# The first load of a gated linear unit issued before the launch barrier in place of after it

## The chip, the cores and the metric

The kernel runs on one core of one Trainium2 chip. The metric is the device time of one execution in microseconds (us). Each kernel is run several times, and the kernel before is run again in the same rounds.

## The reference, cut to what matters

```python
def setup_inputs():
    return {"x": np.random.randn(8192, 8192).astype(np.float32)}

def reference(x):
    a, b = np.split(x, 2, axis=-1)
    return a * (1 / (1 + np.exp(-b)))      # 8192 x 4096, float32
```

268.44 MB are read and 134.22 MB are written. For each output element there is one sigmoid and one multiply.

## The kernel before

The input is worked in 32 tiles. A tile has two rows of x in each of the 128 partitions (64 KB per partition, 8.4 MB in all), and there are two buffers for the input tile and two for the output tile. SyncE issues the loads, ScalarE computes the sigmoid of the b half in place, VectorE multiplies, ScalarE issues the stores. Only the last tile is worked and stored in four pieces per row.

```python
pool = ctx.enter_context(tc.tile_pool(name="io", bufs=BUFS))        # 2
# ... cut: the variant with one row for each partition, not used ...
for i in range(n_tiles):                                            # 32
    x_sb = pool.tile([P, in_cols], fp32)
    o_sb = pool.tile([P, out_cols], fp32)
    eng(LOAD_ENG, i).dma_start(out=x_sb, in_=x_t[i])                # SyncE
    n_chunks = TAIL_CHUNKS if i >= n_tiles - TAIL_ITERS else 1      # 4 in the last tile
    for r in range(PAIR):                                           # 2
        # ... cut: the slices a_part, b_part, o_part ...
            nc.scalar.activation(out=b_part, in_=b_part, func=SIG)
            nc.vector.tensor_mul(out=o_part, in0=a_part, in1=b_part)
            # ... cut: in the last tile a store for each piece ...
    if n_chunks == 1:
        eng(STORE_ENG, i + 1).dma_start(out=out_t[i], in_=o_sb)     # ScalarE
```

One part of the program is not in this text. The framework puts an entry block ahead of the kernel's own instructions. In it GpSimd fills four small constants, and then all five engines meet at what is called the launch barrier here: each executes a drain (DRAIN in the profile) and signals its arrival through a semaphore, a counter that other engines can wait for; GpSimd waits for the four other arrivals and then releases all. The kernel's first load stands after this barrier.

## Time and profile before

| | before |
|---|---|
| time, median of the first runs | 936.99 us (936.17 to 937.19) |
| span of the profiled execution | 934.1 us |
| DMA engines | 9 tenths or more in 39 of 40 slices, 431 GB/s on average |
| VectorE, ScalarE busy | 30%, 25% |
| issue of the first load | 0.73 us after the start of the span |
| first sigmoid | 22.66 us |

The page of the profiled execution begins with the busy shares, the span in 40 slices (a digit is the busy share in tenths), the bytes moved, and the chain of waits that ended last.

```profile
...
DVE 280.9 (30%) x70; ACT 230.0 (25%) x71; POOL 0.2 (0%) x4
...
DMA  9999999999999999999999999999999999999998
...
DMA packets 10226, 402.67 MB, mean 431 GB/s; under 512 B 1136, under 2 KB 1136, under 8 KB 2160
...
## 4 chain that ended last, share of the span: by engine, by line
DMA 78%; DVE 15%; ACT 6%; issue 0%; DVEq 0%; ACTq 0%; SPq 0%
...
```

The compute engines are mostly idle, the DMA engines hardly ever. The Trainium skill, "DMA: Bandwidth & Descriptors", Specifications, gives a fabric ceiling of 435 GB/s, and the 431 GB/s of this trace agree with it. So the DMA engines bound the kernel, and with the same bytes to move, time can be won only where they are idle. That is at the two ends of the span. The head is the subject here.

This is the order of time of the head in the trace of before (start, duration, engine, line, operation; in brackets the idle time of the engine before it and what ended it).

```profile
...
0.73 1.28 ACT L84 ACT_TABLE_LOAD   x1 [0.73 <-PEq L106]
0.73 34.69 SPq L70 DMA_DIRECT2D x_sb<-in_x_dram  x3
22.66 7.12 ACT L84 ACTIVATE x_sb<-x_sb 128x4096 f32<-128x4096 f32 x2 [20.65 <-DMA x_sb<-in_x_dram]
26.31 8.76 DVE L85 TENSOR_TENSOR o_sb<-x_sb 128x4096 f32<-128x4096 f32 x2 [26.31 <-ACT x_sb L84]
...
```

Nothing is computed before 22.66 us. ScalarE is idle for 20.65 us and waits for the first load to land, that is for its last bytes to be in place.

These are the instructions of the barrier in the same trace. The columns are line, engine, operation, count, then the duration in ns (shortest, median, longest) and the first and the last start in us.

```profile
...
L106 POOLq EVENT_SEMAPHORE  x2: 17/17/17, 0.5 to 0.6; - x2
L106 SPq DRAIN  x1: 7/7/7, 0.0 to 0.0; - x1
...
L106 POOLq DRAIN  x1: 181/181/181, 0.3 to 0.3; - x1
L106 PEldq DRAIN  x1: 8/8/8, 0.3 to 0.3; - x1
...
L106 SPq EVENT_SEMAPHORE  x1: 17/17/17, 0.7 to 0.7; - x1
...
```

SyncE is there first, at 0.0 us. GpSimd, which has the four constants to fill, drains only at 0.3 us and releases the others with its semaphore instructions at 0.5 and 0.6 us. SyncE goes on at 0.7 us. In the view of what the DMA-issuing queue of SyncE waited for, this is the line of the launch (the profile names the engine whose arrival came last by its records, PE).

```profile
...
SPq L106 <- PEq L106: 0.7, 1, 0.7
...
```

So 0.7 us pass in which the core could have fetched data. The last line needed is that of the DMA engines in the first 3 us, in 40 slices of 0.075 us each.

```profile
...
DMA  0000000000000000000000099900909000090000
...
```

The first packets (pieces of a transfer, here 64 KB each) start in slice number 23, counted from zero. The view counts a packet in the slice in which it starts, so the zeros after it are not idle time: the same view gives the time of these 16 packets as 104.9% of the window.

### The profile page before, as it was taken

The page shows a single profiled execution, that of the slowest core. Times are in us where ns is not written, and L with a number is a line of the kernel's source. Part 1 is how long each engine was busy: PE and PEld are TensorE (multiplying, and loading weights), DVE is VectorE, ACT ScalarE, POOL GpSimd, SP SyncE. Part 2 cuts the span into 40 slices and gives each one's busy share as a digit, 9 for nine tenths or more (in the row PEclk, how much of TensorE's full clock was granted, in tenths as well). Part 3 has the DMA queues.
Part 4 walks back from the last instruction along what each step waited for, and adds up shares of the span by engine and source line. Part 5 has one row for each costly group of instructions (what it writes and reads, how often), then busy time and mean ns, then how long its engine had stood idle before and what let it go on. Part 6 is the DMA issues. An engine that isn't in the chain of part 4 may idle for free.

```text
span 934.1 us, 410 instructions
## 1 busy us (share of the span) xinstructions
DVE 280.9 (30%) x70; ACT 230.0 (25%) x71; POOL 0.2 (0%) x4
## 2 busy tenths in 40 slices
DVE  0333321333213332133321333312333123331234
ACT  0313331133311333113332033320233202333023
POOL 0000000000000000000000000000000000000000
DMA  9999999999999999999999999999999999999998
GB/s 404 404 449 427 427 449 427 427 434 464 404 441 434 428 449 425 451 408 462 410 429 446 425 450 420 453 408 453 421 429 446 424 452 429 441 411 450 424 449 359
DMA packets 10226, 402.67 MB, mean 431 GB/s; under 512 B 1136, under 2 KB 1136, under 8 KB 2160
## 3 DMA queue, kind: packets, MB, share of 16 engines
q1 hardware_dynamic: 4608, 268.44, 66.5%
q10 hardware_dynamic: 5616, 134.22, 33.3%
q14 instruction: 2, 0.02, 0.0%
HBM read 268.44 MB, written 134.22 MB: 431 GB/s over the span
## 4 chain that ended last, share of the span: by engine, by line
DMA 78%; DVE 15%; ACT 6%; issue 0%; DVEq 0%; ACTq 0%; SPq 0%
DMA x_sb<-in_x_dram 78%; DVE o_sb L85 15%; ACT x_sb L84 6%; DVEq L117 0%; ACTq L87 0%; SPq L70 0%; ACTq L84 0%
## 5 line engine op out<-in xcount | busy, mean ns | idle before, releaser
L85 DVE TENSOR_TENSOR o_sb<-x_sb 128x4096 f32<-128x4096 f32 (+1 forms) x70 | 280.9, 4056 | 647.3 <-ACT x_sb L84 647.3
L84 ACT ACTIVATE x_sb<-x_sb 128x4096 f32<-128x4096 f32 (+1 forms) x70 | 228.7, 3315 | 696.1 <-DMA x_sb<-in_x_dram 692.0
L84 ACT ACT_TABLE_LOAD x1 | 1.3, 1283 | 0.7 <-PEq L106 0.7
L106 POOL MEMSET const-bfloat16-1.0<- 128x1 bf16 x1 | 0.1, 102 | 0.0
L106 POOL MEMSET const-uint8-127<- 128x1 uint8 x1 | 0.1, 102 | 0.0
L106 POOL MEMSET const-float32-1.0<- 128x1 f32 x1 | 0.1, 99 | 0.0
L106 POOL MEMSET const-float32-0.0<- 128x1 f32 x1 | 0.1, 98 | 0.2 <-issue 0.2
## 6 DMA issues: line engine op xcount, KB each, us to landing
out_dram<-o_sb ACTq DMA_DIRECT2D x31, 4096.0 KB, 41.8
out_dram<-o_sb ACTq DMA_DIRECT2D x8, 512.0 KB, 6.3
x_sb<-in_x_dram SPq DMA_DIRECT2D x32, 45.5
```

What stands on the lines that cost most here:

```text
L84: nc.scalar.activation(out=b_part, in_=b_part, func=SIG)
L85: nc.vector.tensor_mul(out=o_part, in0=a_part, in1=b_part)
L106: nc = _bacc.Bacc("TRN2", target_bir_lowering=False, num_devices=1)
```

## The change

The intent is to issue the first load while the engines are still gathering. It has no input that the barrier protects and it waits for no semaphore. The source was rewritten without its dead options at the same time. The core of the diff, with the rewritten loop cut, is this:

```diff
 ... cut: the loop, rewritten as _tiles() with the same tiles, buffers and queues ...
+    with ExitStack() as pools:
+        _tiles(pools, tc, x, out)
+    tc.close()
+    tc.compile()
+    blocks = nc.main_func.blocks
+    entry, body = blocks[0].instructions, blocks[1].instructions
+    SP = mybir.EngineType.SP
+    at = next(k for k, i in enumerate(body) if i.engine == SP)
+    load = body[at]
+    assert load.opcode == "DMACopy" and not load.sync_info.on_wait
+    del body[at]
+    where = next(k for k, i in enumerate(entry) if i.engine == SP and i.opcode == "Drain")
+    entry.insert(where, load)
```

More of the change, by code (lines that the diff above doesn't have):

```diff
@@ L1 @@
-import os
 from contextlib import ExitStack
@@ L5, with _tiles @@
 import concourse.tile as tile
-from concourse import bass_utils, mybir
+from concourse import mybir
 from concourse._compat import with_exitstack
+def _tiles(ctx, tc, x, out):
+    nc = tc.nc
+    P = nc.NUM_PARTITIONS
+    fp32 = mybir.dt.float32
+    SIG = mybir.ActivationFunctionType.Sigmoid
+    n_rows, n_cols = x.shape
+    half = n_cols // 2
+    R = 2
+    n_tiles = n_rows // (P * R)
+    x_t = x.rearrange("(n p r) m -> n p (r m)", p=P, r=R)
+    out_t = out.rearrange("(n p r) m -> n p (r m)", p=P, r=R)
+    pool = ctx.enter_context(tc.tile_pool(name="io", bufs=2))
+    first = None
+    for i in range(n_tiles):
+        x_sb = pool.tile([P, R * n_cols], fp32)
+        o_sb = pool.tile([P, R * half], fp32)
+        load = nc.sync.dma_start(out=x_sb, in_=x_t[i])
+        first = first or load
+        n = 4 if i == n_tiles - 1 else 1
+        w = half // n
+        for r in range(R):
+            for c in range(n):
+                lo = r * n_cols + c * w
+                a = x_sb[:, lo : lo + w]
+                b = x_sb[:, lo + half : lo + half + w]
+                cols = slice(r * half + c * w, r * half + (c + 1) * w)
+                nc.scalar.activation(out=b, in_=b, func=SIG)
+                nc.vector.tensor_mul(out=o_sb[:, cols], in0=a, in1=b)
+                if n > 1:
+                    nc.scalar.dma_start(out=out_t[i, :, cols], in_=o_sb[:, cols])
+        if n == 1:
+            nc.scalar.dma_start(out=out_t[i], in_=o_sb)
+    return first
 @with_exitstack
@@ L17 @@
     nc = tc.nc
-    P = nc.NUM_PARTITIONS
-    PAIR = int(os.environ.get("GLU_PAIR", "2"))
-    BUFS = int(os.environ.get("GLU_BUFS", "2" if PAIR == 2 else "5"))
-    STORE_ENG = os.environ.get("GLU_STORE", "scalar")
-    LOAD_ENG = os.environ.get("GLU_LOAD", "sync")
-    TAIL_CHUNKS = int(os.environ.get("GLU_TAIL_CHUNKS", "4"))
-    TAIL_ITERS = int(os.environ.get("GLU_TAIL_ITERS", "1"))
-    n_rows, n_cols = x.shape
-    half = n_cols // 2
-    assert out.shape == (n_rows, half)
-    fp32 = mybir.dt.float32
@@ L32 @@
-    SIG = mybir.ActivationFunctionType.Sigmoid
-    def eng(name, i):
-        if name == "alt":
-            name = "sync" if (i % 2 == 0) else "scalar"
-        return getattr(nc, name)
-    pool = ctx.enter_context(tc.tile_pool(name="io", bufs=BUFS))
-    if PAIR == 1:
-        x_t = x.rearrange("(n p) m -> n p m", p=P)
-        out_t = out.rearrange("(n p) m -> n p m", p=P)
-        n_tiles = x_t.shape[0]
-        for i in range(n_tiles):
-            x_sb = pool.tile([P, n_cols], fp32)
-            eng(LOAD_ENG, i).dma_start(out=x_sb, in_=x_t[i])
-            n_chunks = TAIL_CHUNKS if i >= n_tiles - TAIL_ITERS else 1
-            csz = half // n_chunks
-            for c in range(n_chunks):
-                lo = c * csz
-                hi = lo + csz
-                a_part = x_sb[:, lo:hi]
-                b_part = x_sb[:, half + lo : half + hi]
-                nc.scalar.activation(out=b_part, in_=b_part, func=SIG)
-                nc.vector.tensor_mul(out=a_part, in0=a_part, in1=b_part)
-                eng(STORE_ENG, i + 1).dma_start(out=out_t[i, :, lo:hi], in_=a_part)
-    else:
-        x_t = x.rearrange("(n p r) m -> n p (r m)", p=P, r=PAIR)
-        out_t = out.rearrange("(n p r) m -> n p (r m)", p=P, r=PAIR)
-        n_tiles = x_t.shape[0]
-        in_cols = PAIR * n_cols
-        out_cols = PAIR * half
-        for i in range(n_tiles):
-            x_sb = pool.tile([P, in_cols], fp32)
-            o_sb = pool.tile([P, out_cols], fp32)
-            eng(LOAD_ENG, i).dma_start(out=x_sb, in_=x_t[i])
-            n_chunks = TAIL_CHUNKS if i >= n_tiles - TAIL_ITERS else 1
-            for r in range(PAIR):
-                a_all = x_sb[:, r * n_cols : r * n_cols + half]
-                b_all = x_sb[:, r * n_cols + half : (r + 1) * n_cols]
-                o_all = o_sb[:, r * half : (r + 1) * half]
-                csz = half // n_chunks
-                for c in range(n_chunks):
-                    lo = c * csz
-                    hi = lo + csz
-                    a_part = a_all[:, lo:hi]
-                    b_part = b_all[:, lo:hi]
-                    o_part = o_all[:, lo:hi]
-                    nc.scalar.activation(out=b_part, in_=b_part, func=SIG)
-                    nc.vector.tensor_mul(out=o_part, in0=a_part, in1=b_part)
-                    if n_chunks > 1:
-                        eng(STORE_ENG, i + 1).dma_start(
-                            out=out_t[i, :, r * half + lo : r * half + hi], in_=o_part
-                        )
-            if n_chunks == 1:
-                eng(STORE_ENG, i + 1).dma_start(out=out_t[i], in_=o_sb)
```

## The prediction

> **What bounds the kernel now.** The 16 DMA engines. The page's slices show DMA at 9 tenths in 39 of 40 slices; 402.67 MB moved at a mean of 431 GB/s. VectorE is busy 30% of the 934.1 us span, ScalarE 25%. The Trainium skill, "DMA: Bandwidth & Descriptors", Specifications, gives a fabric ceiling of 435 GB/s; the 431 GB/s agree. The chain that ended last is 78% loads and 21% the sigmoid and multiply between a load's landing and the next load into the same buffer, but while that chain is in VectorE the other buffer's load and the stores fill the DMA engines.
>
> **What the change does.** Arithmetic, tiles, buffers, queues and tail are the same. One instruction moves: the first load goes from behind the launch barrier to before SyncE's drain, which is SyncE's arrival at it.
>
> Sizes, from the instructions of the barrier's line and of the load's line. SyncE's drain is at 0.0 us, so SyncE reaches the barrier first; PE's and GpSimd's drains are at 0.3 us (GpSimd's takes 0.18 us, after four memsets), GpSimd's two semaphore instructions are at 0.5 and 0.6, and SyncE's release is at 0.7. The first load is issued at 0.73 us, its issue takes about 0.4 us (0.417 is the longest of the 32), and the data phase starts at 1.17 us in the chain of waits. All of this heads the chain: the sigmoid waits until 22.66 us for that load.
>
> Removed: at most 0.73 us, the release at which the first load stands. Added: SyncE's arrival at the barrier comes about 0.4 us later, but still before GpSimd's chain at 0.5 us, so the barrier should end where it did, or 0.1 us later. Moved: the second load is issued as the first instruction of SyncE after the barrier, at about 0.75 us instead of 1.15; it queues behind 8.4 MB that need about 20 us. ScalarE's table load stays at 0.73 us and ends at about 2.0. A drain doesn't wait for data: ScalarE's last one took 0.15 us while its stores needed about 6 us to land, so SyncE's should not wait for the load either.
>
> **How much shows.** All work after the first landing only follows its predecessors, so the whole schedule should be shifted, by 0.6 to 0.75 us: about 0.07%. The three runs of before spread over 1.0 us, so the gain is smaller than the spread of single runs.
>
> **Prediction.** 936.3 us, 8 in 10 between 934.9 and 937.4. Faster by over 2%: 0.005; within 2%: 0.99; slower by over 2%: 0.005.
>
> **What would show the steps right.** The first load's issue at 0.0 us; the data phase at about 0.45 us; the first sigmoid at about 21.95 us in place of 22.66; the barrier's release still at 0.7 to 0.8 us; the last multiply about 0.7 us earlier; load landings still 45.5 us (median), sigmoid 3.6 us and multiply 4.42 us, the same rate of about 431 GB/s; span about 933.4 us.
>
> **What would make it wrong.** The span's zero is the first instruction: if SyncE starts no earlier in real time and its first issue is slower, the gain shrinks to nothing. If SyncE's drain did wait for the data, the second load would be issued at about 22 us and the DMA engines would idle some 2 us between the two: slower by about 1 us. A different interleaving of loads and stores could move the total by a microsecond either way.

## The result, and the profile after

The changed kernel took 935.99 us (median of 5 runs, 935.59 to 936.31), against 936.99 us before (936.17 to 937.19, 5 runs). The ratio is 0.9992, with a 95% interval from 0.9980 to 1.0004; it is the mean time of one kernel's runs over that of the other's in the same rounds, so it is not quite the ratio of the medians. By its interval this pair alone does not tell a gain from none. Executions over 1.5% slower than the fastest of the same kernel are left out of the means. All outputs are right. The changed kernel's span is 933.9 us.

The page of the profiled execution after, with the lines that answer to those of before:

```profile
...
DVE 280.9 (30%) x70; ACT 230.0 (25%) x71; POOL 0.2 (0%) x4
...
DMA  9999999999999999999999999999999999999998
...
DMA packets 10226, 402.67 MB, mean 431 GB/s; under 512 B 1136, under 2 KB 1136, under 8 KB 2160
...
DMA 78%; DVE 15%; ACT 6%; issue 0%; DVEq 0%; ACTq 0%
...
```

None of these totals changed. The order of time of the head after:

```profile
...
0.00 34.73 SPq L28 DMA_DIRECT2D x_sb<-in_x_dram  x3
...
0.78 1.28 ACT L38 ACT_TABLE_LOAD   x1 [0.78 <-PEq L85]
21.96 7.12 ACT L38 ACTIVATE x_sb<-x_sb 128x4096 f32<-128x4096 f32 x2 [19.90 <-DMA x_sb<-in_x_dram]
25.61 8.76 DVE L39 TENSOR_TENSOR o_sb<-x_sb 128x4096 f32<-128x4096 f32 x2 [25.61 <-ACT x_sb L38]
...
```

The first load is issued at 0.00 us and the first sigmoid starts at 21.96 us in place of 22.66. The barrier's instructions after:

```profile
...
L85 POOLq EVENT_SEMAPHORE  x2: 17/17/17, 0.6 to 0.7; - x2
...
L85 POOLq DRAIN  x1: 181/181/181, 0.3 to 0.3; - x1
...
L85 SPq DRAIN  x1: 126/126/126, 0.4 to 0.4; - x1
L85 SPq EVENT_SEMAPHORE  x1: 17/17/17, 0.7 to 0.7; - x1
...
```

SyncE now drains at 0.4 us, behind the issue of the load. That drain takes 126 ns in place of 7, but it does not wait for the 8.4 MB, and GpSimd's release moves by less than 0.1 us. In the waits of SyncE's queue 0.2 of the 0.7 us are left:

```profile
...
SPq L85 <- PEq L85: 0.2, 1, 0.2
```

The DMA engines in the first 3 us after the start:

```profile
...
DMA  0000000000000999909900000000090000000000
...
```

The first packets start in slice 13, ten slices sooner than before. The same view of a window of 0.2 us, with finer slices, puts them at 1.00 us, and in before at 1.73: 0.73 us sooner. The Trainium skill, "DMA: Bandwidth & Descriptors", Latency and other measured facts, gives about 0.6 us to the first byte on the path that SyncE uses. The load's issue takes 0.376 us here, so the first packet comes 0.6 us after the end of the issue, which agrees, but 1.0 us after its start.

One thing in this pair of profiles does not fit a plain shift. These are the first sigmoids of the last tile, in the order of time of before and then of after:

```profile
...
914.83 2.95 ACT L84 ACTIVATE x_sb<-x_sb 128x1024 f32<-128x1024 f32 x3 [21.79 <-DMA x_sb<-in_x_dram]
...
914.69 2.95 ACT L38 ACTIVATE x_sb<-x_sb 128x1024 f32<-128x1024 f32 x3 [21.76 <-DMA x_sb<-in_x_dram]
...
```

The gain is 0.70 us at the first sigmoid of the kernel and only 0.14 us here (the expectations call this the last sigmoid), and the spans differ by 0.2 us. The median of five says 1.0 us. Whether the gain is kept, and whether it is the load's at all, had to be tried.

### The profile page after: what moved, and what is told of

Its sections match the earlier page's. It is cut to its first block, busy times and chain, and to the rows that moved or that the text cites. A ratio compares the mean times of both kernels' runs of the same rounds, so it can differ in the third digit from the quotient of the medians.

```text
span 933.9 us, 410 instructions
## 1 busy us (share of the span) xinstructions
DVE 280.9 (30%) x70; ACT 230.0 (25%) x71; POOL 0.2 (0%) x4
## 4 chain that ended last, share of the span: by engine, by line
DMA 78%; DVE 15%; ACT 6%; issue 0%; DVEq 0%; ACTq 0%
DMA x_sb<-in_x_dram 78%; DVE o_sb L39 15%; ACT x_sb L38 6%; DVEq L61 0%; ACTq L41 0%; ACTq L38 0%
```

## The experiments

Theory: only the start of the first load matters, and an earlier start shifts the whole schedule, because the DMA engines are busy from then on. Rivals: the difference comes from the rewrite or from chance; or the gain is used up in the saturated middle; or the second load's earlier issue has a part in it.

### The move undone, and the changed kernel again (e1, e2)

Kernel e1 is the changed kernel without the edit of the blocks. The built program has, instruction for instruction, those of before. Kernel e2 is the changed kernel.

```diff
-    blocks = nc.main_func.blocks
-    entry, body = blocks[0].instructions, blocks[1].instructions
-    ...
-    entry.insert(where, load)
```

> The rewritten source with the first load left behind the barrier. Theory (the move alone makes the gain, about 0.7 us, and it shifts the whole schedule): same as the kernel before, ratio within 0.9996 to 1.0004, first sigmoid at 22.6 to 22.7 us. Rival (the rewrite or the chip made the 1.0 us difference of the medians): the time of the changed kernel, about 0.999, although the first sigmoid stands at 22.66.

> The changed kernel once more, in the rounds of the undone one. Theory: 0.6 to 0.8 us under before and under the undone kernel (ratio 0.9991 to 0.9994), first sigmoid at 21.95 us, and the gain at the last sigmoid scattered around 0.7 us. Rival (the gain at the head is used up later by the saturated DMA engines, as the first pair of profiles suggests, 0.70 us at the first sigmoid and 0.14 at the last): first sigmoid at 21.95 us, but again only 0.0 to 0.3 us at the last one and in the time.

Measured: e1 936.42 us (median of 5; ratio to before 0.9997), first sigmoid at 22.50 us. Kernel e2 936.04 us (ratio 0.9992), first sigmoid at 21.96 us. Kernel before in the same rounds 936.75 us (9 runs). The means of the runs are 936.52, 936.05 and 936.77 us. The sign is the theory's, but not all that was expected came: e2 lies 0.72 us under before but only 0.47 under e1, e1's first sigmoid is 0.1 us sooner than expected, one run of e2 took 936.97 us, and e1 lay 0.25 us under a kernel with the same instructions. In the profile of e2 the last tile's first sigmoid starts at 914.73 us, only 0.10 us before that of before, as the rival said, and 0.30 before that of e1 (915.03). One profile of each is too little here. Over all kept profiles with the short barrier the load behind it gives 914.83 (before), 915.03 (e1) and 915.54 (e9), and the load ahead of it 914.69, 914.73 (e2) and, from experiments below, 914.30 (e5), but also 917.16 (e10). So before is the earliest of its kind, all profiles but e10 keep some of the gain to the last tile, and e10 is looked at below. At this size repetition alone answers slowly.

### The barrier made longer by a known amount (e3, e4)

If the load's place counts, then a longer barrier must make the difference larger. Ten memsets on GpSimd go ahead of its drain in the entry block, once in the undone kernel (e3) and once in the changed one (e4). The edit, shortened:

```diff
+    pad = ctx.enter_context(tc.tile_pool(name="pad", bufs=1)).tile([P, 1024], fp32)
+    for _ in range(10):
+        nc.gpsimd.memset(pad, 0.0)
 ...
+    for p in pads:                  # the ten memsets, taken out of the body
+        at = next(k for k, i in enumerate(entry) if i.engine == POOL and i.opcode == "Drain")
+        entry.insert(at, p)
```

> First load behind the barrier, and the barrier made longer by 10 memsets of 128x1024 on GpSimd ahead of its drain. They delay the release by D, to be read in this trace (D guessed at 10 us, between 5 and 20). Theory: the time grows by all of D, since the first load waits for the release: before plus D within 0.5 us. Rival (a delay at the head is used up later): clearly less than D.

> First load ahead of the same longer barrier. Theory: D is hidden whole as long as the release comes before the first load has landed (about 22 us), as the second load still queues behind the first: the time of the changed kernel within 0.5 us, that is D plus 0.7 us under the padded undone kernel; first sigmoid at about 22 us. Rival (the load's early start is worth only its own fixed 0.7 us, or the data does not flow before the barrier is over): the time grows by part or all of D.

The order of time of e3, load behind the barrier:

```profile
...
0.37 10.03 POOL L26 MEMSET pad<- 128x1024 f32 x10
...
10.71 34.57 SPq L31 DMA_DIRECT2D x_sb<-in_x_dram  x3
32.51 7.12 ACT L41 ACTIVATE x_sb<-x_sb 128x4096 f32<-128x4096 f32 x2 [20.53 <-DMA x_sb<-in_x_dram]
...
```

And of e4, load ahead of it:

```profile
...
0.00 56.23 SPq L31 DMA_DIRECT2D x_sb<-in_x_dram  x4
...
0.36 10.03 POOL L26 MEMSET pad<- 128x1024 f32 x10
...
21.87 7.12 ACT L41 ACTIVATE x_sb<-x_sb 128x4096 f32<-128x4096 f32 x2 [9.89 <-DMA x_sb<-in_x_dram]
...
```

In both the memsets run to about 10.4 us. In e3 the first load is issued at 10.71 us, 9.98 us later than in before, and the first sigmoid starts at 32.51. In e4 it is issued at 0.00 and the first sigmoid starts at 21.87 us, though SyncE stood 10.1 us at the barrier by its own waits:

```profile
...
SPq L95 <- PEq L95: 10.1, 1, 10.1
...
```

The times: e3 946.52 us (4 runs, ratio 1.0105), e4 936.03 us (5 runs, ratio 0.9992). The delay of 9.98 us costs e3 10.1 us against the mean of the undone kernel in the same rounds (946.58 less 936.52), and costs e4 nothing (936.00 against 936.05 for e2). Between e3 and e4 lie 10.58 us, where the first loads are issued 10.71 us apart. This is the finding that carries the rest, as it is far outside the scatter (the five runs of e1 lie within 0.66 us, those of e2 within 1.52): a delay of the first load of this size shifts the end one to one within about 0.1 us, nothing of it that these runs can tell is given back in the middle, and a load ahead of the barrier hides this barrier whole.

### Two loads ahead of the barrier (e5)

The edit is the same insertion, done twice.

> The first two loads both ahead of the short barrier. Theory (only the start of the first load matters; the second queues behind it for 20 us): the time of the changed kernel, ratio to before 0.9990 to 0.9996, first sigmoid at 21.9 to 22.0 us, second at 43.5 to 43.8; the barrier may end 0.3 us later, since SyncE now issues for about 0.8 us before its drain, and nothing shows of it. Rival (the second load's earlier issue is part of the gain): a further gain of about 0.4 us.

Measured: 935.68 us (5 runs, ratio 0.9992), first sigmoid at 22.03 us, second at 44.07. Their mean lies 0.81 us under before of the same rounds, and those of the changed kernel's first two sets 0.82 and 0.72 us under theirs. No further gain shows. The release moved to 1.25 us, 0.5 us later than in the changed kernel where 0.3 was expected, and both sigmoids are a little later than expected, the second by 0.3 us; none of this shows in the time.

### Where the hiding ends (e6, e7, e11)

The same memsets, 40 of them, with one load ahead of the barrier (e6) and with two (e7).

> First load ahead of a barrier of 40 memsets; release at about 40.6 us (10 memsets made 9.97 us). Theory: hiding ends where the first load has landed, at 21.9 us. The DMA engines idle from then to the issue of the second load at 40.6 us, 18.7 us: time of the changed kernel plus 18 to 20 us, about 955 us, in place of plus 40 where the load stands behind the barrier. First sigmoid at about 42 us, after the table load. A theory in which any barrier is hidden: plus 0. One in which only the head of the load is hidden: plus 39.

> Two loads ahead of the same 40 us barrier. Theory: the DMA engines work until both have landed at 43.5 us. The first sigmoid starts at about 42 us (table load after the release), so the first store and the third load are issued when VectorE has done the first tile, 12.4 us later, at about 54.4 us in place of 34.4. Idle DMA from 43.5 to 54.4 us, so plus 10 to 12 us: about 947 us. If the second load ahead of the barrier brings nothing, the time of the run with one load, about 955.

In the order of time of e6, these are the table load after the release and the first sigmoid:

```profile
...
40.95 1.28 ACT L41 ACT_TABLE_LOAD   x1 [40.95 <-PEq L95]
42.24 7.12 ACT L41 ACTIVATE x_sb<-x_sb 128x4096 f32<-128x4096 f32 x2
...
```

The stretches of e6 from 20 to 41 and from 41 to 42 us; the last two figures of a line are the share of the DMA engines and GB/s:

```profile
...
20.00:41.00 21.00, 0.00 (x0) 0.05 (x1) 19.49 (x21) 1.00 0.00 0
41.00:42.00 1.00, 0.00 (x0) 1.00 (x1) 0.00 (x0) 1.00 1.00 328
...
```

The first load landed at 21.9 us and the next packets come after 41 us. For some 20 us (21.9 to 41.9) the DMA engines have nothing to move. Kernel e6 took 956.79 us (2 runs), which is 20.8 us more than the changed kernel, against the 18 to 20 expected. What was short in the sum: the release came at 40.9 us in place of 40.6, and the second load needs another microsecond from its issue to its first packet. With both the sum is 20 us; the other 0.8 us is no more than single runs of other sets scatter, and its cause is not shown.

The two early loads of e7 are both issued within 0.4 us of the start. Their times from issue to landing:

```profile
...
DMA to landing us min/median/max: 22.0/31.4/40.8
```

The stretches of e7 between the second landing and the first store and third load:

```profile
...
41.00:55.00 14.00, 8.76 (x2) 8.39 (x3) 0.00 (x0) 1.00 0.00 0
55.00:56.00 1.00, 0.00 (x0) 0.86 (x1) 0.00 (x0) 1.00 2.82 786
...
```

Two loads with nothing beside them land at 40.8 us. The 43.5 us of the expectation were read from the changed kernel, where a third load and a store share the DMA engines from 34.4 us on. That made the idle stretch 14.8 us in place of 11. Kernel e7 took 954.01 us in its one fast run, 18.0 us more than the changed kernel, so 3 us beyond the idle stretch; its other run, 968.60 us, is listed as slow because it lies over 1.5% above the first, not for its granted clock, which is 1.0 too. It was run again:

> Two loads ahead of the 40 us barrier again, as one of its two runs was slow. The first profile had both loads landed at 40.8 us, since alone they are not slowed by a third load and a store as in the changed kernel (43.6), and the first packet after the release at 55.6 us: 14.8 us idle. Theory: plus 15 to 18 us, 951 to 954 us, and at least 2 us under the run with one load ahead (956.8). If that one fast run was a chance: 947 as first expected.

Four runs, on another chip, took 961.83 to 967.60 us. So five of the six runs of this program lie above the two of e6 with one early load (956.64 and 956.95), and the 954.01 is the exception. A profile of e7 (that run) and one of e11 say where they part. The bytes moved by e7 from the start to 470 us, from the view of the DMA queues for that window:

```profile
...
DMA packets 4383, 196.00 MB, mean 417 GB/s; under 512 B 480, under 2 KB 480, under 8 KB 480
...
```

The same for e7 to 900 us:

```profile
...
DMA packets 8654, 382.65 MB, mean 425 GB/s; under 512 B 958, under 2 KB 958, under 8 KB 958
...
```

For e11 to 470 us:

```profile
...
DMA packets 4381, 195.96 MB, mean 417 GB/s; under 512 B 480, under 2 KB 480, under 8 KB 480
...
```

And for e11 to 900 us:

```profile
...
DMA packets 8534, 378.16 MB, mean 420 GB/s; under 512 B 928, under 2 KB 928, under 8 KB 928
...
```

Up to 470 us they agree within 0.04 MB, and both are 7 MB, or 16 us, behind the changed kernel, which had moved 202.92 MB by then. That is the cost of the head. After about 620 us the tiles of e11 come every 29.8 to 30.6 us in place of 29.0, with the DMA engines busy throughout. What slows them there is not known, and the kernel's total is not used for a verdict: the expectation of 951 to 954 us was missed, and the claim that a second early load is worth something beside a 40 us barrier stands only on the head of the traces (7 MB behind at 470 us with two loads, 9.4 MB with one). By the clock it was a loss in five runs of six.

### The other end of the kernel (e8)

The head suggests that the tail be looked at in the same way. The last load becomes two, one for each row, so that the first row is worked while the second still loads, and SyncE issues the stores of the last tile. The edit, shortened:

```diff
-        load = nc.sync.dma_start(out=x_sb, in_=x_t[i])
+        for r in range(R):          # in the last tile only
+            row = slice(r * n_cols, (r + 1) * n_cols)
+            load = nc.sync.dma_start(out=x_sb[:, row], in_=x_t[i, :, row])
-                    nc.scalar.dma_start(out=out_t[i, :, cols], in_=o_sb[:, cols])
+                    nc.sync.dma_start(out=out_t[i, :, cols], in_=o_sb[:, cols])
```

> The changed kernel with the other end of the same chain mended: the last load is two loads, one for each of the tile's two rows, and the eight stores of the last tile are issued by SyncE, so that ScalarE no longer stands in its queue behind stores that wait for VectorE (2.05 us, twice). From the profile of the changed kernel: between the last load's landing at 914.6 us and the last store's at 930.6 the DMA engines move 4.2 MB, which take 9.7 us at 431 GB/s, so about 6 us of 16 are idle. Theory: 3 to 5 us less than the changed kernel, 931 to 933 us. If the tail is bound by the stores themselves: under 1 us.

Measured: 935.81 us (5 runs), with a mean 0.84 us under before of the same rounds, which is what the changed kernel's first two sets gained without this edit (0.82 and 0.72). So the expectation of 3 to 5 us was wrong. The DMA engines of the changed kernel from 914.6 us, the last load's landing, to 930.6:

```profile
...
DMA  1991991991991991389999999999999999999999
...
DMA packets 1147, 6.53 MB, mean 408 GB/s; under 512 B 126, under 2 KB 126, under 8 KB 1065
...
q10 hardware_dynamic: 1147, 6.53, 97.6%
...
```

They are busy: the last line gives the time of these packets as 97.6% of the window (the digits count a packet where it starts). They move 6.53 MB in this stretch and not the 4.2 MB of the last tile: the store of the tile before, issued at 898 us, is far from done when the last load lands. The mistake was to count only the bytes issued after a landing. As long as older transfers are in flight, an earlier tail only changes whose bytes come first.

### The scatter (e9, e10, e12)

The undone and the changed kernel were run once more.

> The undone kernel once more, as its first five runs lay 0.3 us under before although its instructions are the same. Theory (the move alone): together with the first five, within 0.3 us of before, first sigmoid 22.5 to 22.7 us. Rival (part of the gain comes with the rewrite): again 0.3 us or more under before.

> The changed kernel in the same rounds. Theory: the mean of its runs 0.5 to 0.9 us under that of before and of the undone kernel; first sigmoid at 21.96 us. Rival (given back later): under 0.3 us.

Kernel e9 took 936.61 us (mean 936.57, that of before in the same rounds 936.62): together with e1 the undone kernel lies 0.15 us under before of the same rounds on the mean, so the rewrite itself gives nothing that these runs can tell. Kernel e10 took 936.75 us, with runs from 935.93 to 937.90 us and a mean 0.17 us over before. This set missed the expectation. Its profile has the early head (first sigmoid at 21.97 us), but the second load landed 2.4 us later than in the first profile of the changed kernel (second sigmoid at 46.04 us against 43.68), the last tile's first sigmoid came at 917.16 us against 914.69, and in its tail there is a hole. The DMA engines from 917 us to 935, in slices of 0.45 us:

```profile
...
DMA  5993959933999999987999999992039999940000
...
```

From slice 27 to 29, that is from 929.2 to 930.5 us, they have almost nothing to do. The stores of the last pieces are not there yet. Up to 914 us this run had moved as many bytes as the first profile (395.43 MB), so the DMA engines had lost nothing before; that another order of loads and stores brought the last load late is inferred, not shown. The hole leaves about 1 us open at the end, and the profiled time is 1.25 us over that of the first profile (937.24 against 935.99). If only this costs the slower runs their time, the mended tail of e8 must be free of them:

> The kernel with the mended tail once more. Of 15 runs of the changed kernel four lay 0.7 to 1.9 us above the middle; the profile of one of them had the last load's landing 2.5 us later than usual, with as many bytes moved by 914 us as usual, and the DMA engines short of stores only after it. Theory (an order of loads and stores that lands the loads later costs time only through the tail behind the last landing): the mended tail, whose first half is worked while the second half still loads, has no such runs: all five under 936.5 us, mean 935.5 to 936.1. Rival (the late runs lose DMA time elsewhere): one or two of five over 936.7 us.

It was not: four runs took 935.65 to 936.35 us and one 937.77. The hole is about as large as the delay of the run of e10 that was profiled. It is not shown to be the cause in the others, and what delays single runs by 1 or 2 us stays open.

All runs together are the last evidence. With the first load behind the short barrier there are 51 (before and undone): median 936.80 us, the fastest 936.17. With it ahead and the tail unchanged (the changed kernel three times, e4, e5) there are 25: median 936.03 us, and 18 of the 25 are faster than the fastest of the 51. The medians differ by 0.77 us, the means by 0.59 (936.72 less 936.13; with standard errors of 0.05 and 0.11 us), as four of the 25 are late by 0.7 us or more. The runs are pooled over several chips, so this is a count in support and not a controlled interval. Set by set, against the mean of before in the same rounds, the five sets with the load ahead lie 0.82, 0.72, 0.77 (e4) and 0.81 us (e5) under it and 0.17 us over it (e10); the two undone sets, which are the program of before, lie 0.25 and 0.06 under it. So sets of one and the same program differ by up to 0.25 us, and four sets of five show a gain about three times that.

No version was clearly faster than the changed kernel: e5, e8 and e12 have medians of 935.68 to 935.81 us, within the scatter.

## Why the prediction was right

- **What bounds the kernel.** Right. 431 GB/s and 9 tenths of DMA in 39 of 40 slices, before and after.
- **0.73 us at the head of the chain.** Right. The first load was issued at 0.00 us, the first packets came 0.73 us sooner, the first sigmoid was forecast for 21.95 us and started at 21.96.
- **The barrier ends where it did, or 0.1 us later.** Right. The table load that follows the release moved from 0.73 to 0.78 us.
- **The drain does not wait for the data.** Right. It took 126 ns, though the load needs 21.9 us to land. It was not free as the text may suggest: without an issue before it, it took 7 ns.
- **The data phase at about 0.45 us.** Wrong as put. The 1.17 us, read from the chain, are where the second load's issue begins, as the chain goes through that load; they are not the first packet. The packets began at 1.73 us before and 1.00 us after. The difference of the two, which is what counts, was not touched by that.
- **A shift of the whole schedule by 0.6 to 0.75 us.** Right in kind, and in size as far as these runs can tell. The 10 us barrier shows the shift (9.98 us of delay cost 10.1 us behind the barrier and nothing ahead of it). For the small barrier the pooled medians give 0.77 us and the means 0.59, four sets of five show 0.72 to 0.82, and one (e10) shows no gain. The single pair of profiles did not show it: its last multiply was only 0.1 us earlier and the span 933.9 us, not 933.4. Its time before is likely the fastest of the five (936.17 us, judged by the 2.0 to 2.1 us between time and span in the other runs of before and of the changed kernel), so this pair understates the gain.
- **Time.** 936.3 us forecast, 934.9 to 937.4 the range, 935.99 us measured. This says little for the mechanism: the range also holds all five runs of before (936.17 to 937.19), so a change that did nothing would have landed in it. The steps above are what was tested.

## What to carry to other kernels

Where the DMA engines bound a kernel, look at the ends of the span, because here nearly all the unused time lay before the first packet and after the last. Look before counting on it: at the tail, older stores filled the time that seemed free (e8). A load that waits for nothing can be issued before the launch barrier, and it then hides the barrier for as long as it takes to land; here that turned 0.7 us of 937 into gain, and would turn 10 us into gain if the barrier were that long. A suspected effect below the scatter is tested by making it larger: ten memsets said in one pair of kernels what 76 runs of the short barrier say only in their medians. What the larger barrier shows is the mechanism; the size of the small gain rests on the 0.73 us of the traces and on those 76 runs.

## What the Trainium skill lacked or had wrong

- "DMA: Bandwidth & Descriptors", Latency and other measured facts: the first-byte latency of about 0.6 us does not say from where it counts. In the changed kernel the first packet came 1.00 us after the start of the first load's issue and 0.6 us after its end (issue 0.376 us).
- "DMA: Bandwidth & Descriptors", Where 436 GB/s comes from: the page says that the HBM side, about 358 GB/s, binds transfers between HBM and SBUF. Put so generally it does not hold for one core, as the 425 GB/s that it gives beside it as near the fabric rate already shows. This kernel's mixed reads and writes held 431 GB/s over the whole span, so here the fabric figure was the one to plan with. No run here shows what two cores at once would get.
- "Runtime: NRT & Kernel Launch", The ~15µs preamble/postamble breakdown: the table has the runtime's own barriers, but not the program's own entry barrier, which lies within the measured span. Here it cost 0.73 us, of which GpSimd's four constants and its drain took the first 0.5.
- No page was found that says whether a drain waits for a DMA issued before it. Here SyncE's drain right after the issue took 126 ns in place of 7, while the load needed 21.9 us.
- No page was found with the scatter of a kernel at the bandwidth limit: with the same instructions the tiles came every 29.0 us in most profiles, and every 29.8 to 30.6 us in the last third of one run (e11), at an unchanged granted clock of 1.0.
